# Dealing filler matmuls and early branch weights in the attention stage of a hybrid encoder block

## The chip, the cores and the metric

The kernel runs on one core of a Trainium2 chip. The time is the device time of one execution in microseconds (us). The engines are named as in the profile: PE is TensorE, DVE is VectorE, ACT is ScalarE, POOL is GpSimd, and SP is SyncE, which issues all the DMAs and DMA transposes here, one after the other.

## The reference

One layer of an encoder block on a 16 x 64 grid of tokens (1024 tokens, 1024 channels), in float32.

```python
u = rms_norm(x, norm1_g)
q, k, v, cb, cc, ch, ga, gb = split(u @ w_in)
q, k = rms_norm per head of q, k
y_a = neighbourhood_attention(q, k, v, rpb) @ w_attn_branch   # 8 heads x 64, window 8 x 16
z = cc * ch
conv = zp[:, :-2] * w[0] + zp[:, 1:-1] * w[1] + zp[:, 2:] * w[2]
y_b = (cb * conv) @ w_conv_branch
merged = sigmoid(ga) * y_a + sigmoid(gb) * y_b
x = x + merged @ w_o
x = x + relu(rms_norm(x, norm2_g) @ w_mlp_in) ** 2 @ w_mlp_out
```

## The kernel before

Every float32 operand is scaled by a power of two and split into a high and a low float16 half, and each product is three float16 matmuls (high-high, high-low, low-high). So every weight chunk goes through a preparation (`Chunk.prep`, L250): a largest value or a sum of squares is taken on DVE or ACT, a matmul with ones sums it over the partitions (L198), small DVE operations make the scale, ACT writes the high half and DVE the low one. These preparations are generators in a background list `bg`; `tick` (L152) advances the first of them that does not answer that it waits. `side[0]` lets it look past a waiting one. `flush` and `built` (L169, L183) force them to the end at the point where the weights are due. PE's queue is in the order in which the program emits it, written out by hand, and so are the other engines' queues.

The attention stage is a loop over steps `k` (L1001), N = 64 steps of one head and one block of 128 queries, and 13 more for the end of the pipeline. Step `k` emits the scores of step `k` (two matmuls, `at_qk`, into one of three banks `ps_s`), the addition of the bias with the row maximum on DVE (`at_max`, `sz<-ps_s`) of step k - 1, the high half of the probabilities on ACT (`at_hi`) of k - 4, their low half on DVE (`at_lo`, `P<-sz,sc,P`) of k - 5, at every second step a DMA transpose of the probabilities of two steps (`at_turn`, PT, L878) of k - 6, the exponential on ACT (`at_exp`) of k - 1, and at every fourth step the P·V matmuls (`at_pv`, L905) of k - 12. Other DMA transposes, `turn_piece` (L931), stand in SP's queue at the steps 35 to 58 and 66 to 73.

Between these, `emit` (L922) puts filler matmuls on PE: the 576 matmuls of the generator `conv_mms` (L766), the input projection for the short convolution (four chunks of 144, of which 48 of the first are done ahead of the loop) and half of the first gate (48). Whenever the generator comes to the next chunk it calls `flush`, and pushes the preparation of the chunk after it; at the last conv chunk (j = 3) it also pushes those of the first gate (`cG`) and of the first chunks of the two branch weights (`cA[0]`, `cB[0]`). `share(k)` (L983) says how many fillers step `k` gets. What follows the conv matmuls elementwise is `conv_post`, then `conv_taps`, then `conv_split` (L748), of which the loop advances one piece per step (`deal`, L992).

`V` and `A` are wrapped by `Meter` (L52), which adds up an estimate of each operation's time at program time. `deal` lets the background advance by one tick per step and by up to three more while the estimate of the step is below `room`, which grows with `share(k)`.

The conv-branch weights `cB` wait in `Chunk.largest` until their `ready` is set, since their scale takes the scales of all four conv splits (`rowsB`):

```python
while not self.ready:
    yield WAIT
mul(rm, self.rows, rm)
```

After the loop come the rest of the fillers, the rest of the conv pieces, `built(cG)`, and then `gate_units(0)` (two units of 24 matmuls) and `branch_units(0)` (two units of 12 with the attention weights `w_wa`, two of 12 with the conv weights `w_wb`, L1184).

Of the kernel before, what the change touches and what calls it, by code (L numbers as in the profile page):

```python
# [70 lines left out]
def encoder_block(ctx: ExitStack, tc: tile.TileContext, x, weights, cols, gqk, rel, masks, out):  # L71
    nc = tc.nc
    G, T, SP = nc.gpsimd, nc.tensor, nc.sync
    V, A = Meter(nc.vector, 0.96, 150), Meter(nc.scalar, 1.2, 190)

    base = ctx.enter_context(tc.tile_pool(name="base", bufs=1))
    rawp = ctx.enter_context(tc.tile_pool(name="rawp", bufs=5))
# [35 lines left out]
    def tmp(n=1):  # L113
        return cols_of("tmp", n)

    def at(c, i, n=1):
        return slice(c.start + i, c.start + i + n)

    def mul(a, b, out=None):
        out = out or tmp(a.stop - a.start)  # L120
        V.tensor_tensor(sc[:, out], sc[:, a], sc[:, b], op=OP.mult)
        return out
# [23 lines left out]
    def step(n=1):  # L146
        for _ in range(n):
            for g in list(fg):
                if not advance(g):
                    fg.remove(g)  # L150

    def tick(n=1):  # L152

        for _ in range(n):
            i = 0
            while i < len(bg):
                r = advance(bg[i])
                if not r:
                    bg.pop(i)
                elif r == WAIT and side[0]:  # L160
                    i += 1
                else:
                    break
# [19 lines left out]
    def built(*chs):  # L183

        forced[0] = True
        while not all(ch.split for ch in chs):
            tick()
            step()
        forced[0] = False
# [166 lines left out]
    for (kind, j), pieces in plan():  # L356
        ch = chunks[kind, j] = Chunk(kind, [(nk, sum(n for _, n in cs)) for _, _, nk, cs in pieces],
                                     {"A": "wa", "B": "wb"}.get(kind, "ws"), rows.get(kind, lambda j: g1)(j),
                                     j if kind == "V" else None, 9 if kind in "VQKCGS" else 0)
        ch.first = len(loads)  # L360
        for p, (k, w) in enumerate(ch.widths):
            ch.offs.append(offset)
            if kind != "X" and (kind, j) != ("1", 0) and (kind, j, p) != ("1", 1, 1):
# [3 lines left out]
    cV, cConv, cA, cB, cO, c1, c2, c2x = ([chunks[k, j] for j in range(n)] for k, n in  # L367
                                              (("V", 2), ("C", 4), ("A", 4), ("B", 4), ("O", 2),
                                               ("1", 16), ("2", 4), ("X", 4)))
# [65 lines left out]
    def pow2_half(ss, top, s, inv, more=0):  # L435

        V.tensor_scalar(sci[:, ss], sci[:, ss], EXP, None, op0=OP.bitwise_and)
        yield
        V.tensor_scalar(sci[:, ss], sci[:, ss], 1.0, float(1 << 23), op0=OP.mult, op1=OP.add)
        yield  # L440
        V.tensor_scalar(sci[:, ss], sci[:, ss], 1, EXP, op0=OP.logical_shift_right, op1=OP.bitwise_and)
        yield
        V.tensor_scalar(sci[:, s], sci[:, ss], -1.0, float((190 + top) << 23), op0=OP.mult, op1=OP.add)
        V.tensor_scalar(sci[:, inv], sci[:, ss], 1.0, float((64 - top - more) << 23), op0=OP.mult, op1=OP.add)
        yield
# [131 lines left out]
    for p in range(11):  # L577
# [7 lines left out]
        for q in (p,) if p < 6 else (2 * p - 6, 2 * p - 5):  # L585
            c = q // 2 + 3
# [56 lines left out]
    for n, (kind, b) in enumerate(todo):  # L643
        ch = cQ if kind == "q" else cK
# [60 lines left out]
    def perm(t, half=None):  # L705
        v = t.rearrange("p (r b c) -> p b r c", r=16, b=8)
        return v if half is None else v[:, 4 * half:4 * half + 4]

    def conv_post(j, g, half, ps, d):

        ch = cConv[j]
        p3 = ps.rearrange("p (b r c) -> p b r c", b=4, r=16)
        if g == 0:
            if half == 0:
                d["z"] = w2p.tile([128, S + 2], F32, name="z", bufs=1)
                G.memset(d["z"][:, 0:1], 0.0)
                G.memset(d["z"][:, S + 1:S + 2], 0.0)
            A.activation(perm(d["z"][:, 1:S + 1], half), p3, AF.Copy, scale=sc[:, ch.inv])
            return
        if g == 1:  # L720
            zn = perm(d["z"][:, 1:S + 1], half)
            V.tensor_tensor(zn, p3, zn, op=OP.mult)
            if half == 1:
                d["cv"] = w2p.tile([128, S], F32, name="cv", bufs=1)
                conv_tail.append(conv_taps(ch, d))
            return
        while not d.get("taps"):
            yield
        cv = d["cv"]
        V.tensor_tensor(perm(cv, half), p3, perm(cv, half), op=OP.mult)  # L730
        if half == 1:
            conv_tail.append(conv_split(j, cv))
# [15 lines left out]
    def conv_split(j, cv):  # L748
        ch = cConv[j]
        m, s, inv = tmp(), tmp(), tmp()  # L750
        A.activation(BT[:, 1, j].bitcast(BF16), cv, AF.Square, accum_out=sc[:, m])
        yield
        V.tensor_scalar(sc[:, m], sc[:, m], 1e-36, None, op0=OP.max)
        yield
        yield from pow2_half(m, 14, s, inv)
        mul(inv, ch.inv, at(rowsB, j))
        G.tensor_scalar(cv, cv, sc[:, s], 1.0, op0=OP.mult, op1=OP.mult)
        yield
        bh, bl = (BT[:, w, j].rearrange("p (b r c) -> p b r c", b=8, r=16) for w in range(2))
        A.activation(bh, perm(cv), AF.Copy)  # L760
        yield
        pv = perm(cv)
        for b in range(0, 8, 2):
            G.tensor_tensor(bl[:, b:b + 2], pv[:, b:b + 2], bh[:, b:b + 2], op=OP.subtract)
# [40 lines left out]
    def conv_step(n):  # L805

        conv_live.extend(conv_q)
        conv_q.clear()
        while conv_live and not advance(conv_live[0]):
            conv_live.pop(0)  # L810
        for _ in range(n):
            if conv_tail and not advance(conv_tail[0]):
                conv_tail.pop(0)
# [164 lines left out]
        yield  # L978
        ch.s, ch.inv = yield from scale_of(am, 9, 1)

    meters, debt, mark = (V, A), [0.0, 0.0], [V.ns, A.ns]

    def share(k):  # L983
        return 9 if k < 55 else 5 if k < 67 else 2

    def account(k):
        room = 216.0 * share(k) + 570.0
        for i, m in enumerate(meters):
            debt[i] = min(600.0, max(0.0, debt[i] + m.ns - mark[i] - room))
            mark[i] = m.ns  # L990

    def deal(k):  # L992
        room = 216.0 * share(k) + 570.0
        if conv_tail and not advance(conv_tail[0]):
            conv_tail.pop(0)
        for n in range(4):
            if n and any(debt[i] + m.ns - mark[i] > room - 200.0 for i, m in enumerate(meters)):
                return
            tick(1)

    for k in range(N + 13):  # L1001
# [6 lines left out]
        if ok(0):  # L1008
            at_qk(k)
        emit(min(4, share(k)))  # L1010
        if ok(1):
            at_max(k - 1)
# [27 lines left out]
    emit(1000)  # L1040
    while conv_live or conv_tail or conv_q:
        conv_step(1)
    for ch in cB:
        ch.ready = True
    built(cG)
    p2.close()
    pbias.close()

# [825 lines left out]
```

## Time and profile before

| | us |
|---|---|
| median of 3 runs (lowest, highest) | 1239.75 (1237.73, 1241.18) |
| the profiled execution | 1236.77 |
| its span, first to last instruction | 1235.0 |
| attention loop in it, first scores to first gate unit | 166.1 to 337.3 |

In rows of the time order, the first number is the start in us from the start of the span, the second the duration, then the engine, the line, the operation, what it writes and reads, and how many of them are merged; in brackets stands the idle time of the engine in front of it and what ended it. Rows of waits name the waiting group, what it waited for, the total in us, how often, and the longest. Rows of stretches give the stretch and its length, then the busy time of PE, its weight loads, DVE, ACT and POOL with the number of instructions, PE's granted clock (1.00 is full), the share of the DMA engines and GB/s. L66 is the decorated meter's line: nearly all DVE and ACT instructions go through it, so these are told apart by their tiles.

### The profile page before, as it was taken

The page shows a single profiled execution, that of the slowest core. Times are in us where ns is not written, and L with a number is a line of the kernel's source. Part 1 is how long each engine was busy: PE and PEld are TensorE (multiplying, and loading weights), DVE is VectorE, ACT ScalarE, POOL GpSimd, SP SyncE. Part 2 cuts the span into 40 slices and gives each one's busy share as a digit, 9 for nine tenths or more (in the row PEclk, how much of TensorE's full clock was granted, in tenths as well). Part 3 has the DMA queues.
Part 4 walks back from the last instruction along what each step waited for, and adds up shares of the span by engine and source line. Part 5 has one row for each costly group of instructions (what it writes and reads, how often), then busy time and mean ns, then how long its engine had stood idle before and what let it go on. Part 6 is the DMA issues. An engine that isn't in the chain of part 4 may idle for free.

```text
span 1235.0 us, 16691 instructions
## 1 busy us (share of the span) xinstructions
PE 1196.9 (97%) x6102; PEld 576.9 (47%) x6102; DVE 936.9 (76%) x1747; ACT 765.9 (62%) x1185; POOL 430.3 (35%) x289
## 2 busy tenths in 40 slices
PE   5989999999899999999999999999999999999998
PEld 3534445555444444444458444444444444444444
DVE  6668778888558786877878664555547999999997
ACT  6777667768644454535768777777775763646430
POOL 2440003232212111101003466655648373463562
PEclk8999999999899999999999999999999999999999
DMA  6558455565761211216096653454474844435202
GB/s 258 107 200 178 103 118 112 116 153 105 131 154 34 69 52 51 69 35 255 18 174 152 205 170 137 162 187 142 140 290 162 313 155 159 168 116 222 103 35 103
DMA packets 170867, 173.34 MB, mean 140 GB/s; under 512 B 131488, under 2 KB 132000, under 8 KB 166688
## 3 DMA queue, kind: packets, MB, share of 16 engines
q1 hardware_dynamic: 170784, 172.27, 47.2%
q8 instruction: 48, 0.79, 0.3%
q14 instruction: 35, 0.29, 0.1%
HBM read 102.51 MB, written 37.75 MB: 114 GB/s over the span
## 4 chain that ended last, share of the span: by engine, by line
PE 40%; DVE 6%; ACT 2%; issue 2%; DMA 1%; DVEq 0%; ACTq 0%
PE ps_d L207 16%; PE ps_s L207 14%; PE ps_o L207 10%; DVE as L66 1%; DVE ops L66 1%; DVE w L66 1%; DVE form L66 1%; ACT as L66 1%; DVE v L66 1%; DMA u2T<-v 1%; DMA u2x<-v 1%; ACT ops L66 1%; DVE x L66 0%; DVE sc L66 0%; ACT u2x L66 0%
## 5 line engine op out<-in xcount | busy, mean ns | idle before, releaser
L207 PEld LDWEIGHTS <-ops 128*128 128x128 f16 x1356 | 132.4, 98 | 159.9 <-issue 2.7
L207 PEld LDWEIGHTS <-w 128*128 128x128 f16 x1368 | 132.8, 98 | 143.5 <-issue 3.8
L924 PE MATMUL ps_d<-uT,w_ws 128*128 128x512 f16 x576 | 136.7, 382 | 0.0
L207 PE MATMUL ps_s<-ops 128*128 128x512 f16 (+1 forms) x528 | 118.3, 374 | 0.0
L207 PE MATMUL ps_d<-ops 128*128 128x512 f16 x504 | 115.6, 379 | 0.0
L66 ACT ACTIVATE ops<-hf,sc 128x2048 f16<-128x2048 f32 x26 | 52.0, 1999 | 94.0 <-PE ps_d L207 52.7
L207 PE MATMUL ps_d<-u2T,w 128*128 128x512 f16 (+1 forms) x504 | 110.3, 371 | 0.0
L1074 POOL TENSOR_TENSOR tsum<-raw 128x512 f32<-128x512 f32 x28 | 46.6, 1677 | 148.1 <-ACT raw L66 148.1
L207 PEld LDWEIGHTS <-uT 128*128 128x128 f16 x648 | 64.9, 101 | 70.5 <-issue 5.6
L1278 POOL TENSOR_TENSOR as<-as 128x512 f32<-128x512 f32 x56 | 76.7, 1370 | 41.4 <-ACT as L66 38.1
L207 PEld LDWEIGHTS <-w_s 128*128 128x128 f16 x588 | 56.9, 98 | 68.6 <-DVE w_s L66 0.6
L924 PEld LDWEIGHTS <-w_ws 128*128 128x128 f16 x576 | 56.1, 98 | 59.7 <-issue 2.0
L207 PE MATMUL ps_s<-u2x,w 128*128 128x512 f16 (+1 forms) x348 | 78.6, 375 | 0.0
L207 PE MATMUL ps_o<-ops 128*128 128x512 f16 x324 | 74.3, 379 | 2.4 <-DVE as L66 2.4
L66 DVE SCALAR_TENSOR_TENSOR ops<-hf,sc,ops 128x2048 f16<-128x2048 f32 x26 | 71.7, 2759 | 5.7 <-ACT ops L66 5.7
L66 ACT ACTIVATE raw<-raw,sc 128x256 f32<-128x256 f32 x172 | 71.1, 494 | 6.7 <-DMA raw<-in_weights 6.7
L66 DVE TENSOR_TENSOR as<-ps_s,as 128x512 f32<-128x512 f32 (+1 forms) x38 | 23.4, 616 | 58.5 <-ACT as L66 57.9
L66 DVE TENSOR_SCALAR sc<-sc 128x1 int32<-128x1 int32 (+3 forms) x380 | 57.6, 167 | 12.9 <-ACT sq L66 4.3
L1074 POOL TENSOR_TENSOR gsum<-raw 128x512 f32<-128x512 f32 x14 | 18.5, 1340 | 136.8 <-issue 52.3
L66 ACT ACTIVATE w<-raw,sc 128x512 f16<-128x512 f32 (+1 forms) x29 | 25.4, 920 | 50.8 <-DVE sc L66 50.8
L66 ACT ACTIVATE sz<-sz,sc 128x384 f32<-128x384 f32 (+1 forms) x64 | 37.2, 581 | 26.8 <-DVE sc L66 26.6
L66 DVE SCALAR_TENSOR_TENSOR w_ws<-raw,sc,w_ws 128x512 f16<-128x512 f32 (+2 forms) x72 | 48.5, 712 | 6.7 <-ACT w_ws L66 6.7
(261 smaller groups left out, 2548.6 us busy)
## 6 DMA issues: line engine op xcount, KB each, us to landing
raw<-in_weights SPq DMA_DIRECT2D x89, 512.0 KB, 5.5
hs<-as SPq DMA_DIRECT2D x16, 1792.0 KB, 8.7
hf<-hs SPq DMA_DIRECT2D x26, 1024.0 KB, 6.7
w2x<-in_weights SPq DMA_DIRECT2D x16, 512.0 KB, 8.3
raw<-in_weights SPq DMA_DIRECT2D x16, 384.0 KB, 3.7
xt<-in_x SPq DMA_DIRECT2D x8, 512.0 KB, 9.8
gs<-s SPq DMA_DIRECT2D x4, 1024.0 KB, 6.4
x<-in_x SPq DMA_DIRECT2D x8, 512.0 KB, 10.0
```

Of the source, the lines that this page charges most:

```text
L66: return f(out, *a, **kw)
L207: T.matmul(ps, l, r, start=a, stop=b)
L924: T.matmul(ps, l, r, start=a, stop=b)
L1074: G.tensor_tensor(t[:, o], a, b, op=OP.add)
L1278: sub.tensor_tensor(z[o], z[a], z[b], op=op)
```

## The change

The fillers' shares by step are dealt anew: from 9, 5 and 2 (steps below 55, below 67, and after) to 9, 8, 6, 7 and 4 (below 6, 55, 64, 73, and after). The conv-branch weights are set ready inside the last conv split, as soon as its scale is emitted, instead of after the loop. The metering wrappers are put on only ahead of the attention loop and taken off behind it.

```diff
-    V, A = Meter(nc.vector, 0.96, 150), Meter(nc.scalar, 1.2, 190)
+    V, A = nc.vector, nc.scalar
...
         mul(inv, ch.inv, at(rowsB, j))
+        if j == 3:
+            for c in cB:
+                c.ready = True
         G.tensor_scalar(cv, cv, sc[:, s], 1.0, op0=OP.mult, op1=OP.mult)
...
-    meters, debt, mark = (V, A), [0.0, 0.0], [V.ns, A.ns]
+    meters = V, A = Meter(nc.vector, 0.96, 150), Meter(nc.scalar, 1.2, 190)
+    debt, mark = [0.0, 0.0], [0.0, 0.0]
 
     def share(k):
-        return 9 if k < 55 else 5 if k < 67 else 2
+        return 9 if k < 6 else 8 if k < 55 else 6 if k < 64 else 7 if k < 73 else 4
...
     while conv_live or conv_tail or conv_q:
         conv_step(1)
-    for ch in cB:
-        ch.ready = True
     built(cG)
+    V, A = nc.vector, nc.scalar
```

## The prediction

> **What bounds the kernel now.** I read the busy shares first, then what TensorE (PE) waited for, then the stretches around the end of attention, and last the order of time there.
>
> ```profile
> span 1235.0 us, 16691 instructions
> PE 1196.9 (97%) x6102; PEld 576.9 (47%) x6102; DVE 936.9 (76%) x1747; ACT 765.9 (62%) x1185; POOL 430.3 (35%) x289
> ```
> ```profile
> PE ps_o L198 <- DVE ones L66: 13.5, 3, 9.5
> PE ps_o L905 <- DMA PT<-P: 5.8, 3, 3.0
> ...
> PE ps_d L207 <- ACT w_wb L66: 1.5, 1, 1.5
> ```
>
> PE is busy for 1196.9 of 1235.0 us, so its queue is the kernel's length, and a change can win only what PE idles or runs slowly: 38 us in all. The longest wait (13.5 us, the start) is not touched. The change lies beside the second and the third: the P·V matmuls of attention wait 5.8 us for their transposed probabilities (PT), and the first use of the conv-branch weights waits 1.5 us.
>
> ```profile
> core 0: us, PE busy (x) PEld busy (x) DVE busy (x) ACT busy (x) POOL busy (x), PEclk, DMA share, GB/s
> 315.00:320.00 5.00, 4.64 (x42) 2.57 (x41) 4.23 (x15) 4.22 (x11) 0.00 (x0) 1.00 0.84 183
> 320.00:325.00 5.00, 2.84 (x14) 1.08 (x11) 3.59 (x19) 5.00 (x14) 0.09 (x1) 1.00 0.79 150
> 325.00:330.00 5.00, 4.21 (x31) 2.53 (x32) 1.71 (x4) 4.97 (x10) 3.32 (x5) 0.66 1.01 119
> 330.00:335.00 5.00, 2.51 (x21) 1.49 (x20) 0.31 (x2) 0.39 (x3) 0.61 (x2) 0.76 0.63 128
> 350.00:355.00 5.00, 3.48 (x17) 1.38 (x15) 2.04 (x8) 1.07 (x3) 0.00 (x0) 1.00 0.81 191
> ```
> ```profile
> 300.06 2.11 PE L924 MATMUL ps_d<-uT,w_ws 128*128 128x512 f16 x9
> ...
> 302.33 1.24 PE L924 MATMUL ps_d<-uT,w_ws 128*128 128x512 f16 x5
> ...
> 311.57 1.01 PE L905 MATMUL ps_o<-PT,vT 128*64 128x256 f16 x18
> ...
> 314.33 0.38 PE L828 MATMUL ps_s<-kD,qD 128*128 128x256 f16 x2 [0.21 <-DVE sc L66]
> ...
> 315.63 0.38 PE L828 MATMUL ps_s<-kD,qD 128*128 128x256 f16 x2
> 315.85 2.32 PE L924 MATMUL ps_d<-uT,w_ws 128*128 128x512 f16 x10
> 318.53 1.18 PE L905 MATMUL ps_o<-PT,vT 128*64 128x256 f16 x24 [0.36 <-DMA PT<-P]
> 319.64 3.19 PE L924 MATMUL ps_d<-uT,w_ws 128*128 128x512 f16 x14
> 325.79 2.13 PE L905 MATMUL ps_o<-PT,vT 128*64 128x256 f16 x24 [2.96 <-DMA PT<-P]
> 327.86 2.53 PE L924 MATMUL ps_d<-uT,w_ws 128*128 128x512 f16 x8
> 332.88 1.81 PE L905 MATMUL ps_o<-PT,vT 128*64 128x256 f16 x18 [2.49 <-DMA PT<-P]
> 334.62 2.56 PE L924 MATMUL ps_d<-uT,w_ws 128*128 128x512 f16 x8
> ...
> 337.26 5.34 PE L207 MATMUL ps_o<-uT,w_ws 128*128 128x512 f16 x24
> ```
>
> Call the loop's steps k. The row at 315.63 is the last score matmul (k = 63); after it stand only fillers (L924) and P·V (L905) until the gate units begin at 337.26. The idle times in brackets add up to 0.21 + 0.36 + 2.96 + 2.49 = **6.0 us**. Behind the two long ones PE is also slow: the granted clock is 0.66 and 0.76. One filler at full clock is (2.11 - 1.24) / 4 = 0.2175 us, so 8 take 1.24 + 3 x 0.2175 = 1.89 us; they took 2.53 and 2.56 (+0.64, +0.67). P·V took 2.13 for 1.18 and 1.81 for 1.01 (+0.95, +0.80). That is **3.1 us** of low clock, 9.1 us with the idle time.
>
> **The change part by part.** *The metering* adds no instruction and removes none. The counters are read only in the attention loop, as differences, and start there at zero either way: nothing.
>
> *The fillers.* 576 matmuls are dealt. Before: 9 x 55 + 5 x 12 + 2 x 10 = 575, one left over. After: 9 x 6 + 8 x 49 + 6 x 9 + 7 x 9 = 563 by k = 72, and the last 13 in the four steps of share 4. Before, 4 x 5 + 10 x 2 + 1 = 41 of them follow the last scores (10 + 14 + 8 + 8 + 1 in the rows). After: 6 + 63 + 13 = 82, the 41 more being taken from the steps 6 to 54. The sum of PE work is the same. The last scores come earlier by 49 x 0.2175 = 10.7 us, less 8 x 0.2175 = 1.7 us for one filler more in the steps 55 to 62, and the 0.2 us wait: about 306.5. Then P·V of k = 68 stands at 306.5 + 0.2 + 6 x 0.2175 + 5 x 7 x 0.2175 + 1.1 (one P·V) = 316.7, and P·V of k = 72 at 316.7 + 1.1 + 4 x 7 x 0.2175 = 323.9.
>
> Are the transposes there by then?
>
> ```profile
> 321.46 0.62 DVE L66 SCALAR_TENSOR_TENSOR P<-sz,sc,P 128x384 f16<-128x384 f32 x1 [0.58 <-ACT P L66]
> ...
> 326.23 3.38 SPq L931 DMA_TRANSPOSE qD<-gs  x2
> 326.24 0.47 DVE L66 SCALAR_TENSOR_TENSOR P<-sz,sc,P 128x256 f16<-128x256 f32 x1
> ...
> 329.66 1.31 SPq L878 DMA_TRANSPOSE PT<-P  x1
> ```
> ```profile
> DMA to landing us min/median/max: 3.0/3.7/5.5
> ```
>
> The low half of step 59 is made at 321.46, 5.8 us after the last scores, and that of step 63 at 326.24, 10.6 us after. If VectorE (DVE) trails by as much as now, step 59 is done at 306.5 + 5.8 + 0.6 = 312.9 and its PT lands 3.7 us later, 316.6 against 316.7. Step 63 is done at 317.6; its transpose also stands in SP's queue behind the two pieces of k = 66 and 67 (L931), which hold it from 326.7 to 329.66 now, and lands 3.2 us after its issue: 317.6 + 3.0 + 3.2 = 323.8 against 323.9. Both just fit: the 6.0 us of idle time go, and with them the 3.1 us. I leave 0.4 us for a near miss. SP's order by step stays; four steps ask of it two PT transposes (1.3 us each by the last row) and one or two pieces (3.38 / 2 = 1.7 us each), 6 us of the 9 that four shorter steps last.
>
> What this costs: the steps 6 to 54 are 0.2175 us shorter, and DVE must follow.
>
> ```profile
> 166.10:337.30 171.20, 165.18 (x1048) 84.20 (x1047) 135.15 (x404) 123.61 (x291) 40.95 (x56) 0.98 0.60 122
> ...
> 219.00:239.00 20.00, 20.00 (x125) 10.03 (x124) 18.80 (x44) 14.31 (x33) 6.44 (x9) 1.00 0.60 138
> 260.00:283.80 23.80, 23.80 (x144) 11.92 (x142) 21.61 (x52) 18.11 (x42) 6.45 (x9) 1.00 0.67 166
> ```
> ```profile
> 237.46 0.60 DVE L66 CUSTOM_DVE_ANT_0 sz<-ps_s,biasm,sc 128x384 f32<-128x384 f32 x1
> ```
> ```profile
> 239.15 0.38 PE L828 MATMUL ps_s<-kD,qD 128*128 128x256 f16 x2
> ```
> ```profile
> 283.21 0.61 DVE L66 CUSTOM_DVE_ANT_0 sz<-ps_s,biasm,sc 128x384 f32<-128x384 f32 x1
> ...
> 283.88 0.38 PE L828 MATMUL ps_s<-kD,qD 128*128 128x256 f16 x2
> ```
>
> Scores have three banks, so those of step k wait until DVE has read step k - 3. DVE is busy for 79% of the whole stage, and for 94% and 91% of the two stretches in it. Scores 30 (239.15) start 1.1 us after DVE let go of 27 (237.46 + 0.6), scores 48 (283.88) only 0.06 to 0.14 us after 45. Over the 8 steps of the first stretch PE gains 1.7 us on DVE, 0.6 more than the margin; over the 10 of the second 2.2, some 2.0 more. So 2.6 us come back as short waits. Bounds: nothing, if the smaller room (2298 instead of 2514 ns) spreads background work over the two more steps that each conv section now has (sections start at k = 11, 29, 47 instead of 10, 26, 42); 49 x 0.2175 = 10.7 us, if DVE can go no faster at all. I take 2.6, from the margins; with the 0.4 above, +3.0.
>
> *The branch weights.*
>
> ```profile
> 352.80 0.17 PE L198 MATMUL ps_d<-ones 128*128 128x1 bf16 x1
> ...
> 353.93 1.71 ACT L66 ACTIVATE w_wb<-raw,sc 128x256 f16<-128x256 f32 x4 [5.42 <-DVE sc L66]
> ...
> 354.49 2.85 PE L207 MATMUL ps_d<-bT,w_wb 128*128 128x512 f16 x12 [1.52 <-ACT w_wb L66]
> ```
>
> Now the sum over the partitions (352.80) is forced out only when the weights are due. With the scales of all four conv splits known at k = 74, the product, the maximum and its copy (three small DVE operations) are issued in the loop, where DVE has no scores left; the sum on PE goes behind the first gate unit, the five small DVE operations and the split (1.7 us on ScalarE) behind the next two, before the 48 matmuls of the gate units and 24 of the attention branch end (72 x 0.2175 = 15.7 us). The wait of 1.52 us goes; next are the weights of the following gate unit, behind these in the same background order, and so not later than now. The raw load that the split releases keeps its place behind the transposes on SP. The conv split itself moves to k = 68 to 76, right to the loop's end; the same 15.7 us lie between it and its reader, and if they did not hide it, its rest (two operations of GpSimd) would be waited for. Bounds: 0 and 1.5; I take 1.5.
>
> **Sum:** -6.0 - 3.1 + 3.0 - 1.5 = **-7.6 us**. The profiled execution took 1236.77 us (span 1235.0 and 1.8 around it), so 1229.2 there; the median shown is 1239.75, 3.0 above it, so **1232** as a median.
>
> [...]
>
> **The rivals.** *DVE is the bound.* For it speak the 94% and 91%, against it that DVE is idle for 36 of the stage's 171 us and that the meter then deals less background work. Then all 10.7 us come back: -9.1 + 10.7 - 1.5 = about 0, 1240.
>
> *The last wait stays.* SP's two pieces hold the last transpose, DVE is some microseconds later than now: 2.49 + 0.80 + 0.67 = 4.0 us stay, the forecast becomes -3.6, 1236.
>
> *Slower: lumps at the section starts.* Each start forces out whatever background work is left.
>
> ```profile
> 273.41 1.14 DVE L66 SCALAR_TENSOR_TENSOR w_ws<-raw,sc,w_ws 128x384 f16<-128x384 f32 x2 [0.16 <-ACT w_ws L66]
> ```
>
> The last conv weights are split at 273.41, right at the third section's start. With less room per step more is left over, and comes in one lump in front of the scores. From a gap of some 2.5 us on, the clock falls as well: 3.1 us for the two gaps of the tail, 1.5 each. Three starts of 2.9 + 1.5 us, beside the 2.6 of short waits: -10.6 + 13.2 + 2.6 = +5, 1245. Against it: two more steps per section, and no gap at any section start now. [...]
>
> **How the numbers follow.** Forecast 0.60, last wait stays 0.14 (half of it beyond 0.3%), DVE the bound 0.13, lumps 0.13. About 0.3% (3.7 us) is what a measurement can tell from no change: faster 0.67, same 0.07 + 0.13 = 0.20, slower 0.13. Range: with no new wait -10.6 us, 1229, and 2 us of spread between runs (1237.73 to 1241.18 shown): 1227. Upwards it takes in DVE as the bound: 1240; the lumps are left out.
>
> **What would show it.** Right: no idle time over 0.5 us at L905 behind the last scores and a clock of 1.00 there; gate units starting some 6 us earlier than 337.26 (9.1 less 3.0); no wait at the first bT matmul; short waits of the scores for DVE around the steps 28 to 32 and 46 to 50, of 2 to 3 us in all. Wrong: score waits of over 5 us, a clock below 1.00 inside the loop, a PT wait over 2 us, or a new wait at the second gate unit's weights.

## The result, and the profile after

| | before | after |
|---|---|---|
| median of 4 runs each (lowest, highest), us | 1239.47 (1237.73, 1241.18) | 1232.76 (1232.41, 1234.81) |
| the profiled execution, us | 1236.77 | 1232.41 |
| its span, us | 1235.0 | 1230.6 |

The ratio of the times is 0.9949 with a 95% interval of [0.9932, 0.9967]: 6.3 us faster (4.1 to 8.4). The forecast was 1232.

The head of the page and the waits of PE in the kernel after:

```profile
span 1230.6 us, 16688 instructions
PE 1197.8 (97%) x6102; PEld 575.8 (47%) x6102; DVE 943.2 (77%) x1747; ACT 765.9 (62%) x1185; POOL 432.5 (35%) x289
```
```profile
PE ps_o L198 <- DVE ones L342: 13.2, 2, 9.6
...
PE ps_d L927 <- DVE cv L66: 2.0, 1, 2.0
...
PE ps_d L198 <- DVE ones L940: 1.3, 2, 0.7
```

The 5.8 us for PT and the 1.5 us for `w_wb` are in no row any more. No score matmul waits. In their place stands one wait of 2.0 us of a filler (L927; the lines of the loop are 3 higher now) for `cv`, and 1.3 us in two sums (L198) that come later. The time order of PE at the end of the loop:

```profile
307.00 0.38 PE L831 MATMUL ps_s<-kD,qD 128*128 128x256 f16 x2
...
310.11 1.18 PE L908 MATMUL ps_o<-PT,vT 128*64 128x256 f16 x24
...
312.10 0.17 PE L198 MATMUL ps_d<-ones 128*128 128x1 bf16 x1
312.13 3.83 PE L927 MATMUL ps_d<-uT,w_ws 128*128 128x512 f16 x17
318.00 1.67 PE L927 MATMUL ps_d<-uT,w_ws 128*128 128x512 f16 x7 [2.04 <-DVE cv L66]
319.60 1.18 PE L908 MATMUL ps_o<-PT,vT 128*64 128x256 f16 x24
...
327.06 1.01 PE L908 MATMUL ps_o<-PT,vT 128*64 128x256 f16 x18
...
330.82 5.34 PE L207 MATMUL ps_o<-uT,w_ws 128*128 128x512 f16 x24
...
346.38 2.75 PE L207 MATMUL ps_d<-bT,w_wb 128*128 128x512 f16 x12
```

The last scores start at 307.00 (315.63 before), none of the three P·V rows behind them has a bracket, and each takes 1.18 or 1.01 us, the time of the full clock. The gate units begin at 330.82 instead of 337.26. The stretches show the same, and what DVE did inside the loop:

```profile
166.28:330.82 164.54, 162.34 (x1048) 82.66 (x1046) 136.18 (x413) 123.40 (x291) 37.48 (x52) 1.00 0.60 127
...
218.00:238.00 20.00, 19.95 (x125) 10.06 (x124) 18.09 (x39) 11.86 (x27) 6.22 (x9) 1.00 0.51 109
257.00:280.50 23.50, 23.50 (x162) 12.28 (x161) 21.18 (x52) 16.41 (x38) 6.22 (x9) 1.00 0.70 157
...
325.00:330.00 5.00, 5.00 (x38) 2.57 (x37) 3.01 (x14) 1.83 (x3) 1.39 (x2) 1.00 0.54 114
```

The loop lasts 164.54 us instead of 171.20. PE's busy time fell by 165.18 - 162.34 = 2.8 us at the same 1048 matmuls, which is low clock that is gone, and its idle time from 6.0 to 2.2.

**Where it went between the two profiled executions.** The loop gives -6.6 us, the way from the first gate unit to the first bT matmul -1.7 (17.23 to 15.56), and the start of the loop lies 0.15 later: -8.1 at 346.38. The span is only 4.4 shorter. What lies between is in two rows of before and three of after:

```profile
712.57 0.16 PE L198 MATMUL ps_s<-ones 128*128 128x1 bf16 x1 [0.79 <-DVE ones L66]
...
948.51 2.75 PE L207 MATMUL ps_o<-ops 128*128 128x512 f16 x12 [2.38 <-DVE as L66]
```
```profile
367.85 0.16 PE L198 MATMUL ps_d<-ones 128*128 128x1 bf16 x1 [0.58 <-DVE ones L940]
...
698.78 4.44 PE L207 MATMUL ps_o<-u2T,w 128*128 128x512 f16 x12 [2.41 <-DVE as L1604]
...
941.60 4.44 PE L207 MATMUL ps_o<-ops 128*128 128x512 f16 x12 [2.39 <-DVE as L1604]
```

The wait at 941.60 is the one of before at 948.51, and as long; but the 12 matmuls behind it take 4.44 us and not 2.75: the clock fell here and did not there. The same holds at 698.78 (its twin of before, at 706.45 behind 2.41 us, took 2.75). So 0.58 + 1.69 + 1.69 - 0.79 = 3.2 us, and 0.69 in another sum at 993.35, were given back behind the change: 3.9, against the 8.1 - 4.4 = 3.7 that are missing. How much of that belongs to the change is asked in the last section.

### The profile page after: what moved, and what is told of

Its sections match the earlier page's. It is cut to its first block, busy times and chain, and to the rows that moved or that the text cites. A ratio compares the mean times of both kernels' runs of the same rounds, so it can differ in the third digit from the quotient of the medians.

```text
span 1230.6 us, 16688 instructions
## 1 busy us (share of the span) xinstructions
PE 1197.8 (97%) x6102; PEld 575.8 (47%) x6102; DVE 943.2 (77%) x1747; ACT 765.9 (62%) x1185; POOL 432.5 (35%) x289
## 4 chain that ended last, share of the span: by engine, by line
PE 40%; DVE 7%; ACT 2%; issue 2%; DMA 1%; DVEq 0%; ACTq 0%
PE ps_d L207 16%; PE ps_s L207 13%; PE ps_o L207 10%; DVE ops L1710 1%; DVE w L1090 1%; DVE form L1281 1%; DVE v L1329 1%; DMA u2T<-v 1%; DMA u2x<-v 1%; DVE ops L1703 0%; DVE x L1464 0%; ACT ops L1701 0%; ACT as L1559 0%; DVE x L1808 0%; DVE as L1603 0%
## 5 line engine op out<-in xcount | busy, mean ns | idle before, releaser
L927 PE MATMUL ps_d<-uT,w_ws 128*128 128x512 f16 x576 | 135.7, 379 | 2.0 <-DVE cv L66 2.0
L927 PEld LDWEIGHTS <-w_ws 128*128 128x128 f16 x576 | 55.6, 98 | 60.7 <-issue 2.6
L959 ACT ACTIVATE raw<-raw,sc 128x256 f32<-128x256 f32 x164 | 67.6, 493 | 11.1 <-DMA raw<-in_weights 11.1
L1594 DVE TENSOR_TENSOR as<-ps_s,as 128x512 f32<-128x512 f32 x13 | 9.0, 691 | 57.9 <-ACT as L1613 57.9
L207 PE MATMUL ps_o<-u2T,w 128*128 128x512 f16 (+1 forms) x204 | 45.9, 376 | 2.4 <-DVE as L1604 2.4
L207 PE MATMUL ps_d<-w_ws,uT 128*128 128x512 f16 x192 | 43.1, 379 | 1.4 <-DVE w_ws L300 1.4
```

Source lines behind the costliest of these rows:

```text
L207: T.matmul(ps, l, r, start=a, stop=b)
L927: T.matmul(ps, l, r, start=a, stop=b)
L959: A.activation(v, v, AF.Copy, scale=sc[:, at(g, 4 * i + k)])
```

## The experiments

"Loop" is the time from the first scores to the first gate unit in the profiled execution: 171.1 us before, 164.5 after. Ratios are against the kernel before on the same chip.

**Which of the three edits?** First the shares alone:

```diff
-        return 9 if k < 55 else 5 if k < 67 else 2
+        return 9 if k < 6 else 8 if k < 55 else 6 if k < 64 else 7 if k < 73 else 4
```

> The new shares alone, the conv-branch weights set ready after the loop as before. If the gain is the sum of two separate parts, this kernel has the whole gain of the attention stage (scores of step 0 to the first gate unit 164.5 us, as after, for 171.1 before) and keeps the wait of about 1.5 us for w_wb: 1.5 us slower than the changed kernel, some 5 us faster than before. If the wait for w_wb is hidden anyway once the loop ends better filled, it is as fast as the changed kernel.

Measured: 1232.92 us, ratio 0.9948 [0.9934, 0.9963], loop 164.6.

```profile
318.19 1.67 PE L924 MATMUL ps_d<-uT,w_ws 128*128 128x512 f16 x7 [2.06 <-DVE cv L66]
331.11 5.34 PE L207 MATMUL ps_o<-uT,w_ws 128*128 128x512 f16 x24
348.34 2.85 PE L207 MATMUL ps_d<-bT,w_wb 128*128 128x512 f16 x12 [1.52 <-ACT w_wb L66]
```

The wait for `w_wb` is untouched, the rest is as in the kernel after: the shares make the whole gain that the times can tell. Then the early branch weights alone:

```diff
         mul(inv, ch.inv, at(rowsB, j))
+        if j == 3:
+            for c in cB:
+                c.ready = True
...
-    for ch in cB:
-        ch.ready = True
```

> The early release of the conv-branch weights alone, the old shares. If the parts are separate: the tail of attention keeps its 9 us (PT waits of about 3.0 and 2.5 us, a low clock behind them) and only the 1.5 us wait for w_wb goes, 1.5 us faster than before, which is hardly to be told from no change. Rival: the earlier preparation gets in the way of the tail, where ScalarE is full, and the PT waits grow by a microsecond or more: no gain or slower.

Measured: 1238.47 us, ratio 0.9990 [0.9977, 1.0003], loop 171.2.

```profile
338.19 5.39 PE L207 MATMUL ps_s<-uT,w_ws 128*128 128x512 f16 x24
...
353.80 2.75 PE L207 MATMUL ps_d<-bT,w_wb 128*128 128x512 f16 x12
```

From the first gate unit to the first bT matmul it is 15.61 us, as after, and there is no bracket: the 1.5 us are gone from the trace. The median is 1.2 us lower, but the interval holds 1, so the time doesn't show it by itself. Last the metering alone:

```diff
-    V, A = Meter(nc.vector, 0.96, 150), Meter(nc.scalar, 1.2, 190)
+    V, A = nc.vector, nc.scalar
...
+    meters = V, A = Meter(nc.vector, 0.96, 150), Meter(nc.scalar, 1.2, 190)
...
+    V, A = nc.vector, nc.scalar
```

> The metering confined to the attention loop, old shares, old release. It changes no instruction, so every theory expects the time of before; what differs is the spread of the measurement.

Measured: 1238.27 us, ratio 0.9996 [0.9985, 1.0008], loop 171.3. Nothing, as argued.

**Is DVE close to being the bound?** One filler less per step in the steps 6 to 54, which go to the end:

```diff
-        return 9 if k < 6 else 8 if k < 55 else 6 if k < 64 else 7 if k < 73 else 4
+        return 9 if k < 6 else 7 if k < 55 else 9 if k < 73 else 4
```

> The changed kernel with 7 fillers instead of 8 in the steps 6 to 54 and 9 in the steps 55 to 72 (6, 7 there before): asks VectorE to go another 0.22 us per step faster. If VectorE has only the margins that the profile of before shows (0.1 and 1.1 us at its tightest places), the scores now wait for it, 5 us or more in all. If the meter hands VectorE less background work and it therefore keeps up, as it did at 8 fillers, the scores wait less than 1 us in all.

Measured: 1234.93 us, ratio 0.9966 [0.9953, 0.9979], loop 165.0.

```profile
192.75 0.48 PE L831 MATMUL ps_s<-kD,qD 128*128 128x384 f16 x2 [1.29 <-DVE sc L66]
...
372.31 0.16 PE L198 MATMUL ps_d<-ones 128*128 128x1 bf16 x1 [4.13 <-DVE ones L940]
```

Even at 7 fillers the scores wait only once, for 1.29 us. So the 91 to 94% of before did not make DVE the bound. How fast it could go with unchanged work this run does not tell, since the meter's room shrinks with the share. A sum at 323.97 waits for another 1.55 us, but the 2.04 us at 318 are not there, and the loop is only 0.4 us longer than after. The 4.13 us at 372.31 lie behind the loop (below). Next, the smaller room is taken away from the meter again, in both places where it is set (one is shown):

```diff
-        room = 216.0 * share(k) + 570.0
+        room = 216.0 * (9 if k < 55 else share(k)) + 570.0
```

> The changed kernel, but the meter's room below step 55 is left at that of 9 fillers (2514 ns instead of 2298), so that as much background work may be issued per step as before. If the scores do not wait in the changed kernel because the meter deals less background work to the shorter steps, they now wait for VectorE, some 2 to 3 us in all. If VectorE simply has more slack than the margins of before seemed to say, there is again no score wait, and the time is that of the changed kernel.

Measured: 1234.92 us, ratio 0.9956 [0.9941, 0.9971], loop 167.1.

```profile
272.30 0.38 PE L831 MATMUL ps_s<-kD,qD 128*128 128x256 f16 x2 [0.81 <-DVE sc L66]
326.19 0.16 PE L198 MATMUL ps_s<-ones 128*128 128x1 bf16 x1 [2.87 <-DVE sc L66]
```

With the old room one score wait of 0.81 us appears, where 2 to 3 us were expected. So the meter, which deals less when the step is shorter, saves 0.8 us of such waits; why the rest of the 2.6 us forecast did not come is not shown. DVE was not far from its limit in the kernel after either: score 31 starts there at 236.53, 0.06 us after DVE let go of score 28 (at 236.47). In front of both score waits, the 1.29 and the 0.81 us, DVE's row for the score stands right behind a split of the next weights (`w_ws`, 1.26 and 0.61 us): background work, but one piece of it and no lump. The 2.87 us at 326.19 belong to a sum whose load is followed further down; here ACT waited 3.35 us for that load.

**What is the new wait of 2.0 us?** The row at 312.10 above is the sum for the attention-branch weights. It takes one of the three PSUM banks of the fillers ("d"), and the fillers go on when DVE has taken a result out of another; in the order of DVE of the kernel after:

```profile
317.27 0.68 DVE L66 TENSOR_TENSOR cv<-ps_d,cv 128x512 f32<-128x512 f32 x1
...
319.62 0.47 DVE L66 SCALAR_TENSOR_TENSOR P<-sz,sc,P 128x256 f16<-128x256 f32 x1
```

The addition ends at 317.95, the filler starts at 318.00. So the sum was put into the banks of the scores:

```diff
-    cG.bank = cA[0].bank = cB[0].bank = "d"
+    cG.bank = cB[0].bank = "d"
+    cA[0].bank = "s"
```

> The changed kernel, but the sum for the first attention-branch weights goes to a score bank (all scores are issued by then) instead of one of the three conv banks. If the new wait of 2.0 us (fillers for VectorE's product of the third conv group) is there because that sum takes up one of three conv banks, it goes. The last P.V then comes 2.0 us earlier, at about 325.0 us, and its transpose, issued at 323.3, lands at about 326.5: 1.5 us come back as a PT wait, and 0.5 us or less is won. If the wait is VectorE's lag alone, it stays.

Measured: 1231.98 us, ratio 0.9934 [0.9919, 0.9949], loop 166.3.

```profile
312.55 0.17 PE L198 MATMUL ps_s<-ones 128*128 128x1 bf16 x1
312.58 5.34 PE L928 MATMUL ps_d<-uT,w_ws 128*128 128x512 f16 x24
...
325.35 0.16 PE L198 MATMUL ps_s<-ones 128*128 128x1 bf16 x1 [2.23 <-DVE sc L66]
```

The wait at 318 is gone, 24 fillers run through; but 2.23 us appear at another sum, 12.8 us later, and the 1.5 us of PT wait that were expected do not. The loop is 1.7 us longer than after, since the clock falls behind the new wait: the ten fillers there take 3.91 us, where ten took 2.32 in the row of before at 315.85. The same with the transposes `turn_piece` three steps later as well (69 to 76):

```diff
-        if 66 <= k < 74:
-            turn_piece(2, 2, k - 66)
+        if 69 <= k < 77:
+            turn_piece(2, 2, k - 69)
```

> As bank, and the eight transposes of the steps 66 to 73 go to the steps 69 to 76, behind the last transpose of probabilities in the queue. If both the bank and the queue hold the tail, neither wait is left: the first gate unit starts 2.0 us earlier than in the changed kernel, and the time is some 2 us less. If the queue does not matter, it is as bank.

Measured: 1232.26 us, ratio 0.9939 [0.9925, 0.9952], loop 164.7. The wait stays (2.27 us at 326.46). I first read this as one lag of DVE that moves from place to place. A later run, below, shows that the second wait has another cause.

**Do the pieces on SP matter?** The later pieces alone, in the kernel before:

> The kernel before with only those eight transposes moved behind the last transpose of probabilities. If SP's queue holds the last transpose for 2.9 us, as read in the prediction, the last PT wait (2.5 us) shrinks to nothing, and the low clock behind it perhaps too: 2.5 to 4 us faster than before. The wait of 3.0 us one P.V earlier stays. If the transpose is late for another reason, both waits stay and nothing is won.

Measured: 1240.08 us, ratio 1.0002 [0.9990, 1.0014], loop 168.0.

```profile
331.81 1.01 PE L905 MATMUL ps_o<-PT,vT 128*64 128x256 f16 x18 [0.76 <-DMA PT<-P]
...
376.34 0.16 PE L198 MATMUL ps_d<-ones 128*128 128x1 bf16 x1 [3.39 <-DVE ones L66]
```
```profile
351.00 0.52 SPq L229 DMA_DIRECT2D raw<-in_weights  x1
351.62 11.80 SPq L1063 DMA_TRANSPOSE uT<-gs  x8
363.52 1.95 SPq L229 DMA_DIRECT2D raw<-in_weights  x4
```

This is a gain that is given back. The last PT wait shrinks from 2.49 to 0.76 and the loop by 3.1 us. But gate 2's second weight load stands in SP's queue behind 8 transposes that hold it for 11.80 us; it is issued at 363.52, and the sum that needs it waits 3.39 us. To test it, the 8 transposes (`turn_s(0, 2)`) were issued behind the attention-branch units, and so behind that load:

```diff
         for g, act, ch in ((0, actA, cA[j]), (1, actB, cB[j])):
             built(ch)
+            if (n, g) == (0, 1):
+                turn_s(0, 2)
...
-            if n == 0:
-                turn_s(0, 2)
```

> As pieces_before, and the eight transposes for gate unit 1 (uT, 11 us of SP's queue) issued one weight load later, just before the conv-branch units, so that the second weight load of gate 2 goes ahead of them. If pieces_before won nothing because its earlier matmuls then waited for that load through SP's queue (a wait of 3.4 us and a slow clock window behind it at 376), this wait goes and the 3 us won in the tail arrive at the end: some 3 us faster than before. If the loss lay elsewhere (the slow clock windows of that one run, say), it is as pieces_before, no change.

Measured: 1235.37 us, ratio 0.9971 [0.9958, 0.9983], loop 168.3.

```profile
350.45 3.27 SPq L229 DMA_DIRECT2D raw<-in_weights  x2
353.82 11.20 SPq L1063 DMA_TRANSPOSE uT<-gs  x8
```
```profile
372.53 0.17 PE L198 MATMUL ps_d<-ones 128*128 128x1 bf16 x1
```

Now both loads go first (x2), the sum at 372.53 has no bracket, and the 3 us of the loop arrive in the time. The slow clock that the expectation puts behind the wait at 376 was not there: the granted clock is 1.00 in 375:380 (last section). The 4.13 us of the kernel with 7 fillers are the same wait (there the eight transposes hold SP for 11.89 us), and the 0.58 at 367.85 in the kernel after is its beginning. So there, too, the transposes were put off, behind the first unit of the attention branch:

```diff
             for half in range(2):
                 ps = anybank()
                 unit(ch_mms(ps, act, half, ch, 4, 256, cc),
                      lambda ps=ps, g=g, half=half, ch=ch: post(g, half, ps, sc[:, ch.inv]), 2, 4)
+                if (n, g, half) == (0, 0, 0):
+                    turn_s(0, 2)
...
-            if n == 0:
-                turn_s(0, 2)
```

> The changed kernel with those eight transposes issued after the first attention-branch unit, one weight load later. If SP's queue is what gate 2 now waits for, the wait of 0.6 us at 367.9 goes, 0.5 us or so faster than the changed kernel, which these rounds can hardly tell; a wait of the fifth matmul group of gate unit 1 for the transposes themselves is the risk, about 1 us.

Measured: 1230.75 us, ratio 0.9931 [0.9911, 0.9950], loop 164.6; the 0.58 us are gone, the 2.05 for `cv` stay. The ratio is 0.0018 below that of the kernel after, but the intervals overlap, so the time does not show it.

**Can the two be had together?** Shares and pieces that leave DVE more room where the sum of `cA` is read:

```diff
-        return 9 if k < 6 else 8 if k < 55 else 6 if k < 64 else 7 if k < 73 else 4
+        return 9 if k < 6 else 8 if k < 55 else 7 if k < 64 else 6 if k < 73 else 4
...
-        if 66 <= k < 74:
-            turn_piece(2, 2, k - 66)
+        if 69 <= k < 77:
+            turn_piece(2, 2, k - 69)
```

> The changed kernel with 7 fillers in the steps 55 to 63 and 6 in the steps 64 to 72 (6 and 7 there), and the transposes of the steps 66 to 73 at 69 to 76: the scores end 1.7 us later, so VectorE, which trails them by 5 us there, has less to catch up. If its lag is the cause of the new 2.0 us wait, that wait shrinks below 0.5 us, the PT does not take its place, and the first gate unit starts 2 us earlier than in the changed kernel: some 2 us faster than it. If it is a matter of the one PSUM bank, the wait stays at 2 us or shows up at another matmul that waits for VectorE.

Measured: 1228.78 us, ratio 0.9916 [0.9897, 0.9934], loop 164.1. In time the best so far, but the loop does not account for it: the first bT matmul comes no earlier than in the kernel after (346.38). In the profiled executions the difference lies behind it, most of it in the waits of 0.58 and 0.69 us, which are missing, and in one stretch of half clock less: behind 2.38 us of idle time at 940.46 the 12 matmuls take 2.75 us, and behind 2.39 us at 941.60 in the kernel after 4.44. No run shows what took these waits away.

```profile
325.40 0.16 PE L198 MATMUL ps_s<-ones 128*128 128x1 bf16 x1 [1.79 <-DVE sc L66]
...
346.57 2.75 PE L207 MATMUL ps_d<-bT,w_wb 128*128 128x512 f16 x12
```

The wait did not fall below 0.5 us either. It stands, with 1.79 us, at the same later sum as in the two kernels with the other bank. This time I followed it back over three engines, PE, DVE and ACT:

```profile
325.00 0.15 DVE L66 TENSOR_REDUCE sc<-sc 128x1 f32<-128x2 f32 x1 [1.88 <-ACT z L66]
```
```profile
319.61 1.71 ACT L66 ACTIVATE raw<-raw,sc 128x256 f32<-128x256 f32 x4 [3.08 <-DMA raw<-in_weights]
...
323.82 1.06 ACT L66 ACTIVATE z<-raw 128x1024 bf16<-128x1024 f32 x1
```

The row of waits names DVE, but DVE had been idle for 1.88 us until ACT had squared the weights (`z<-raw`), and ACT had been idle for 3.08 us until their load landed. Between the load and the last square ACT also did some 1.4 us of other work. This is the scale of gate 2's weights (`scale_s1`), not DVE's lag. In the kernel after, DVE is done with its part at 324.73:

```profile
324.57 0.16 DVE L66 CAST ones<-sc 128x1 bf16<-128x1 f32 x1
```

PE comes to that sum at 324.78, since the wait at 318 has held it up by 2.04 us, and so finds it just ready. That is why the other bank alone won nothing in the loop: the next wait stood right behind the first. The last kernel puts the sum two more background units later, behind the work of 24 more matmuls:

```diff
-        ch.s, ch.inv = yield from scale_of(am, 9, 1)
+        ch.s, ch.inv = yield from scale_of(am, 9, 3)
```

> The kernel p69_76 (shares 9, 8, 7, 6, 4, pieces three steps later) with the sum for the second state weights (S1) put two more background units later on PE; nothing else differs but the turn of the PSUM banks. In p69_76 that sum waits 1.79 us and the profile names DVE, but DVE itself had been idle for 1.88 us until ACT was done with the squares, and ACT had waited 3.08 us for the raw load of S1. Theory A (that load is what the sum waits for): the wait is gone, no wait over 0.3 us takes its place at a sum, P.V of step 72 starts about 325.6 and finds its PT there or waits up to 0.6 us; loop from first scores to first gate unit 162.4 to 162.9 us instead of 164.1; time 0.990 of the kernel before, 1.2 to 1.8 us under p69_76. Theory B (DVE is late with everything at the end of the loop, and whichever comes next waits for it): a wait of 1 to 2 us on DVE or on PT appears behind 320, loop 164, time as p69_76, 0.9916.

Measured: 1227.95 us, ratio 0.9920 [0.9906, 0.9935], loop 162.2.

```profile
167.25 0.38 PE L831 MATMUL ps_s<-kD,qD 128*128 128x256 f16 x2
...
320.35 5.35 PE L927 MATMUL ps_d<-uT,w_ws 128*128 128x512 f16 x24
325.63 1.01 PE L908 MATMUL ps_o<-PT,vT 128*64 128x256 f16 x18
...
329.42 5.34 PE L207 MATMUL ps_s<-uT,w_ws 128*128 128x512 f16 x24
```

No wait is left at the loop's end, and P·V finds its transposes at 325.63. Theory B is refuted, and in the trace theory A came true (a loop of 162.4 to 162.9 us was expected). That the chain starts with the load is read from ACT's row above; no run moved the load itself. In the time the step can't be told: 0.9920 against 0.9916, with intervals of 0.003. The 0.990 that was expected lies outside the interval. The median is 0.8 us below that of the kernel before this one, but the two ran on different chips.

## Why the prediction was right, step by step

Two readings ahead of the sum were wrong, though the sum does not rest on them. The 38 us that a change can win are PE's idle time alone; matmuls at low clock count as busy, so the 3.1 us of low clock stand outside of the 38. And the wait for `w_wb` is the sixth in the list of waits, not the third: 4.8, 2.8 and 2.3 us stand ahead of it.

SP's order in the kernel after, which the first point needs:

```profile
319.42 3.83 SPq L934 DMA_TRANSPOSE qD<-gs  x2
323.29 1.31 SPq L881 DMA_TRANSPOSE PT<-P  x1
```

- **The tail (-6.0 idle, -3.1 clock).** Right in the trace. All three PT waits are gone, and in the loop PE's busy time fell by 2.8 us. As a term of a median the 3.1 is too large: the estimate in the last section is some 2.3. "Both just fit" held for another reason than forecast, and by luck: the low half of step 63 was done at 319.62 + 0.47 = 320.1 and not at 317.6, its transpose left SP behind two pieces, but P·V stood at 327.06 and not at 323.9, since the wait of 2.04 us had moved it too. Less that wait it would have stood at 325.0, and by the 3.2 us of the prediction the transpose lands at 323.29 + 3.2 = 326.5: an estimate of 1.5 us that were hidden and not won. That the pieces hold the last transpose was the rival with 0.14, and its mechanism is real: with the pieces later the wait of before fell from 2.49 to 0.76.
- **The short score waits (+2.6).** Wrong in size: 0 in place of 2.6. The step that failed is to take the margins of 1.1 and 0.1 us as all that DVE had, at unchanged work. All that PE idles in the loop beside the 2.04 us is 0.16 us. The lower bound, where the smaller room spreads background work, explains a part: in 218:238 DVE has 39 instructions (44 in the stretch of the same length before), though in 257:280.5 it has 52 as before, and without the smaller room one wait of 0.81 us comes up. The rest stays open.
- **The near miss (+0.4).** As 2.04 us, at a place that was not named: not PT, but the bank of the fillers. It nearly made up for the step before, so 3.0 given back was measured as 2.0 in the loop and 0.6 at gate 2's sum. The total came out by two errors that cancel, which is luck.
- **The branch weights (-1.5).** Right in the trace (17.23 to 15.56 us, no bracket), in both kernels that have it. By itself too small for the times.
- **The metering (0).** Right.
- **"A new wait at the second gate unit's weights"** was listed as a sign that the prediction is wrong. It came, as 0.58 us, and the runs show the queue behind it.
- **The rivals.** DVE as the bound would have brought 10.7 us back, and lumps at the section starts 13.2. The kernel after has no score wait, and the one with 7 fillers has one of 1.29 us in the whole loop.
- **From trace to median (+3.0).** Taken from before alone. The profiled execution after lies 0.35 us below its median, not 3.0: 1229.2 was forecast for it, and it took 1232.41. So the difference of the profiles (-4.4) is smaller than that of the medians (-6.7), at least in part for the reason that follows, and that the median came so close to 1232 is luck here, too.

## What to carry to other kernels

Fillers are worth most where the last results of a pipeline are awaited; before moving them there, look at what each engine does with a shorter step, and not only at how busy it is, because background work may give way. When a wait is taken out, follow the next one back over all its engines (PE to DVE to ACT to a load) before blaming the one that the profile names, and look at the queue that issues the loads: 3 us won in the loop were lost behind eight transposes. And compare profiled executions with the clock in view: the same idle time of 2.4 us cost 1.69 us more in one of them here than in the other.

## What the runs showed of the hardware

**Idle times of the same length were followed by half clock in one execution and by full clock in another.** In the clock records of the kernel before and of the kernel after, each stretch of half clock between 55 us and the last microseconds lasts 3.41 us (from 325.75 and 332.58 in the one, from 64.67, 699.55 and 941.89 in the other). Ten of the profiled executions (`before`, `after`, `room9`, `bank`, `bank_pieces`, `pieces_before`, `pieces_before_late`, `turn_late`, `p69_76` and `s1_late`) have three idle times of PE of 2.34 to 2.43 us each, near 65, 700 and 945. The row behind took longer in 14 of these 30 cases (7.04 us for 24 matmuls where others took 5.35, or 4.27 to 4.44 for 12 where others took 2.75): in none of the three in the kernel before, in all three in the kernel after. The prediction's "from a gap of some 2.5 us on" does not hold as a threshold: behind 2.23 us in `bank` ten fillers took 3.91 us, behind 2.27 in `bank_pieces` 2.32. The stretch with the twin gaps of 948.51 and 941.60, in the kernel before and in the kernel after:

```profile
940.00:950.00 10.00, 7.62 (x36) 3.32 (x35) 8.40 (x7) 2.54 (x3) 8.15 (x3) 1.00 0.88 328
```
```profile
940.00:950.00 10.00, 8.40 (x32) 3.49 (x32) 4.43 (x8) 7.79 (x6) 4.79 (x4) 0.83 0.20 81
```

The granted clock, the third figure from the end, is 1.00 there and 0.83 here. Even the 3.39 us at 376.34, with the later pieces in the kernel before, left the clock whole (1.00 in 375:380), as did the 0.36 and 1.52 us in the kernel before (1.00 in 315:320 and 350:355):

```profile
375.00:380.00 5.00, 3.66 (x18) 1.68 (x18) 4.79 (x13) 0.00 (x0) 0.00 (x0) 1.00 0.00 0
```

What decides between the two was not shown. But the two stretches of half clock given back in the kernel after do not hang on the change: the kernel before with the pieces and the eight transposes later has both with the old shares (behind 2.41 us at 703.84 and 2.38 at 946.65 PE takes 4.28 and 4.27 us from the start of the 12 matmuls to the start of the next), and the last kernel (`s1_late`), with new ones, has neither (2.58 us each, at 696.94 and at 939.03). Nor was the low clock of the tail a fixed price. The two gaps cost 0.95 + 0.64 = 1.6 us and 0.80 + 0.67 = 1.5 us. All four gaps of 2.87 to 2.98 us in the ten executions had slow matmuls behind them (2.87 in `room9`: 3.62 us for ten fillers; 2.95, 2.96 and 2.98 in `pieces_before`, `before` and `pieces_before_late`: 1.63, 2.13 and 2.13 for a P·V of 1.18); for the one of 2.49 I take the 14 of 30. So I estimate the tail's clock at 1.6 + 1.5 x 14/30 = 2.3 us on average, not 3.1. That these gaps are also what spreads the runs of one kernel was not shown run by run, but it fits: of 29 runs of the kernel before on one chip, the 11 with a mean clock of 0.994 took 1238.1 us on average, the 8 with 0.990 or 0.991 took 1240.4 (the 6 with 0.993 took 1239.1, the 3 with 0.992 took 1241.7).

**The DMA transposes held the queue that issues them.** Eight of them hold SP for 11.2 to 11.8 us in the rows above, 1.4 to 1.5 us each, and with the later pieces in the kernel before the weight load behind them was issued only after 11.80 us, at 363.52; the load ahead of them was itself issued in 0.52 us (the row at 351.00).
